# Raw up-projection weights paired by last use and loaded twice a group, third copies in another ring, operand loads on SyncE's queue

## The chip, the cores and the metric

The kernel runs on one core of a Trainium2 chip. A core has five engines, each with an instruction queue of its own that is worked through in order: TensorE (PE) for matmuls, with weight loads listed as PEld; VectorE (DVE); ScalarE (ACT); GpSimd (POOL); and SyncE (SP), which here only issues DMAs. ACT issues DMAs too; these stand in ACT's own queue between its computing instructions. The metric is device time in microseconds (us), smaller is better.

## The reference

One layer of a hybrid encoder with 2048 tokens of 1024 features, all in float32. With DEPTH = 1 only the GLA mixer runs, then a convolutional FFN:

```python
h = rmsnorm(x, mix_norm_w)
x = x + gla_mixer(h, ...)          # gated linear attention, 4 heads, chunks of 64 tokens
h = rmsnorm(x, ffn_norm_w)
u = causal_dwconv(h @ w_up, conv_w, conv_b)     # 1024 -> 5632, 3 taps over tokens
g, val = split(u, 2)                            # 2816 gate and 2816 value channels
x = x + (silu(g) * val) @ w_down                # 2816 -> 1024
out = rmsnorm(x, final_norm_w)
```

## The kernel before, in words

**Products.** float32 matmuls are made from three matmuls of high and low parts: `mm3p` (L171) issues, for each block of 128 contracted rows, high x low (L176), low x high (L177) and high x high (L178) into one PSUM bank. `split` (L181) makes the parts: ACT copies the source into the high part (L183), DVE subtracts to get the low part (L184). A 2 x 2 block product is done with seven products instead of eight (Strassen-Winograd); they are called p1 to p7, and taken in the order p1, p5, p6, p7, p4, p2, p3 (`OPS`, L86).

**Stages.** The projections of the mixer are done in four passes R, A, B, Y (Y is the out projection), for eight pairs of token tiles each, by `unit`. Pass Y adds x, and `x1_done` and `blocks` normalise and transpose the result for the FFN. For the second half of the tokens (tiles `tt >= 8`) `blocks` stores the transposed tiles to DRAM scratch `h2f` (L762), to be loaded again later. `prep_h2` makes from them the seven operands of the activations, split, and stores these to `hd` (L785). Then `phase_u(s)` is the up projection of token half s, and last the down projection over both halves.

**The up projection.** For a half, `load_op` (L842) loads the split operands of all seven products from `hd` into seven resident tiles, four DMAs of 512 KB for each, as the slot of each comes free (L846): on ACT's queue in half 0, on SP's in half 1. In half 0 these slots hold pass Y's weights until Y's last unit has used them. The weights are taken in 11 groups of two channel tiles (f = 2g and 2g + 1), each with its gate columns f and its value columns NF + f. A job is one product for one channel tile, 12 matmuls; a group has 14 jobs, tile by tile in the order of `OPS`.

The raw weights lie in a ring of four tiles of 512 KB (`raw_tile`). A channel tile's four blocks are a11 and a12 (gate columns, first and second half of the contracted rows) and a21 and a22 (value columns). In the kernel before, one tile holds a11 and a12, another a21 and a22, and `load` (L1011) fetches a group's four tiles with one DMA each (L1016), on SP except for the first group. `prep` makes the split weights of a job, five jobs ahead of its product: p1 from a11; p5 from a21 + a22 (POOL, L1026); p6 from that sum less a11 (L1029), after which a12 less the sum is formed in place (L1044) for p3; p7 from a11 - a21, formed in a21's place (L1032); p4 from a22; p2 from a12. The split weights lie in seven slots, `uw`.

p1, p6, p7 and p4 add up in one PSUM bank `ua`, p5 and p3 in one called `uc`, p2 goes to `ub`. After p1, p6 and p7 ACT copies the bank's running sum out (`copied`, L1049), and the next product of the chain must wait for that copy. The three copies, called c1, c2 and c3, come from the ring `cp` with four slots; c1 is last read after p2 (L1138), c2 after p3 (L1155), c3 right after p7 (L1145). `conv` applies the three taps (L1065 on ACT, L1067 on DVE), and `gated` multiplies gate by value (L1074), forms the operands of the down projection on POOL (L1088 to L1092) in the four-slot ring `as`, and stores them all to `ad` on SP's queue (L1078 to L1094).

**Order.** The kernel is written against a tile framework that makes the semaphores, hands out the slots of each ring and orders each engine's instructions by its own estimate of when each can start; the order in the source is a priority. What it orders on an engine is then fixed: an instruction that waits holds up all behind it on that engine. Some work (`later_do`, `spread`) is written out at times of a planner's clock that advances by 0.227 us a matmul; `spread` puts the steps of `prep_h2` for half 1 between the products of half 0, 11 us apart.

Of the kernel before, what the change touches and what calls it, by code (L numbers as in the profile page):

```python
# [10 lines left out]
F32 = mybir.dt.float32  # L11
# [5 lines left out]
P = 128  # L17
# [3 lines left out]
def f32(ap):  # L21
    return ap.bitcast(F32)
# [3 lines left out]
def hybrid_kernel(  # L26
# [17 lines left out]
    nc = tc.nc  # L44
# [14 lines left out]
    HK = KT // 2  # L59
    NF = F // P  # L60
# [25 lines left out]
    OPS = PORD = ("p1", "p5", "p6", "p7", "p4", "p2", "p3")  # L86
    NQ = NF // 2
# [19 lines left out]
    pools = {}  # L107

    def scratch(shape, name):
        return dr.tile(shape, F32, tag=name, name=name)  # L110
# [6 lines left out]
    h2f = {t: scratch([P, 2, 512], f"h2f_{t}") for t in range(TT, NTT)}  # L117
    wsd = {(ps_, o, k): scratch([P, 2, 512], f"ws_{ps_}_{o}_{k}") for ps_ in "BY" for o in ("p5", "p6", "p7", "p3") for k in range(2)}
    b12d = [scratch([P, 512], f"b12_{j}") for j in range(NP)]
    hd = {(s, o, j): scratch([P, 2, 512], f"hd_{s}_{o}_{j}") for s in range(NS) for o in OPS for j in range(PAIRS)}  # L120
    ad = {(s, o, q): scratch([P, 512], f"ad_{s}_{o}_{q}") for s in range(NS) for o in OPS for q in range(NQ)}

    def mm_ps(name):
        return ps.tile([P, 512], F32, tag="mm", name=name, bufs=4)

    def aux_ps(name):
        return ps.tile([P, 512], F32, tag="aux", name=name, bufs=4)

    def raw_tile(shape, name):
        return wr.tile(shape, F32, tag="raw", name=name, bufs=RB)  # L130

    def w_pair(name):

        return wp.tile([P, 2, 512], F32R, tag="w", name=name, bufs=WB)

    def cp_tile(name):
        return gp.tile([P, 512], F32, tag="cp", name=name, bufs=4)

    def out_tile(name):
        return gp.tile([P, 512], F32, tag="out", name=name, bufs=3)  # L140
# [21 lines left out]
    def need(*what):  # L162

        while not ready.issuperset(what):
            heapq.heappop(delayed)[-1]()
# [15 lines left out]
    def split(hi, lo, src):  # L181

        nc.scalar.copy(hi, src)  # L183
        nc.vector.tensor_sub(lo, src, f32(hi))  # L184
# [563 lines left out]
    def blocks(tt, rws):  # L748

        for k in range(2):  # L750
            pt = aux_ps(f"pt_d{tt}_{k}")
            for j in range(HK):
                kt = HK * k + j
                nc.tensor.transpose(pt[:, j * P:(j + 1) * P], rws[:, kt * P:(kt + 1) * P], ident)
            t = hb2_tile(f"hb2_{tt}_{k}", tt < TT)
            for j in range(HK):
                kt = HK * k + j
                nc.scalar.activation(t[:, j * P:(j + 1) * P], pt[:, j * P:(j + 1) * P], AF.Identity, scale=nw2[:, kt:kt + 1])
            if tt < TT:
                h2[tt, k] = t  # L760
            else:
                nc.sync.dma_start(h2f[tt][:, k, :], t)  # L762
        ready.add(f"h2f{tt}")

    def hb2_tile(name, kept):
        return yp["p"].tile([P, 512], F32, tag="hb2" if kept else "hb3", name=name, bufs=10 if kept else 2)
# [75 lines left out]
    def load_op(s, o):  # L842

        t = uh.tile([P, 2, PAIRS, 512], F32R, tag=o, name=f"h_{s}_{o}", bufs=1)
        for j in range(PAIRS):
            (nc.scalar if s == 0 else nc.sync).dma_start(f32(t[:, :, j, :]), hd[s, o, j])  # L846
        hop[o] = tuple(t[:, i].rearrange("p j (k c) -> p k j c", c=P) for i in range(2))

    ux = {}
# [152 lines left out]
    def tiles1(ap):  # L1002
        return ap.rearrange("p (j k) -> p j k", k=P)

    wuv = w_up.rearrange("(kt p) c -> p kt c", p=P)

    def phase_u(s):
        raws, wops, sums, made = {}, {}, {}, {}
        jobs = [(g, o, f) for g in range(NQ) for o in OPS for f in (2 * g, 2 * g + 1)]

        def load(g):  # L1011
            for f in (2 * g, 2 * g + 1):
                for i, c in enumerate((f, NF + f)):
                    r = raw_tile([P, 2, 512], f"ur_{s}_{c}")
                    q = nc.scalar if s == 0 and g == 0 else nc.sync
                    q.dma_start(r.rearrange("p a (k c) -> p (a k) c", c=P), wuv[:, :, c * P:(c + 1) * P])  # L1016
                    raws[f, i] = r

        def prep(k):
            g, o, f = jobs[k]  # L1020
            a11, a12 = raws[f, 0][:, 0, :], raws[f, 0][:, 1, :]
            a21, a22 = raws[f, 1][:, 0, :], raws[f, 1][:, 1, :]
            add, sub = nc.gpsimd.tensor_add, nc.gpsimd.tensor_sub
            if o == "p5":
                src = sums[f] = out_tile(f"us_{s}_{f}")
                add(src, a21, a22)  # L1026
            elif o == "p6":
                src = sums[f]
                sub(src, src, a11)  # L1029
            elif o == "p7":  # L1030
                src = a21
                sub(src, a11, a21)  # L1032
            elif o == "p3":
                src = sums.pop(f)
            else:
                src = {"p1": a11, "p2": a12, "p4": a22}[o]
            if "wx" in pools and k % (WB + WX) >= WB:
                t = pools["wx"].tile([P, 2, 512], F32R, tag="wx", name=f"uw_{s}_{f}_{o}", bufs=WX)
            else:
                t = w_pair(f"uw_{s}_{f}_{o}")  # L1040
            hl = t[:, 0, :], t[:, 1, :]
            split(hl[0], hl[1], src)
            if o == "p6":
                sub(src, a12, src)  # L1044
            wops[o, f] = hl

        def copied(name, pa):
            t = cp_tile(name)
            nc.scalar.copy(t, pa)  # L1049
            return t  # L1050
# [42 lines left out]
                last = tv  # L1093
                nc.sync.dma_start(ad[s, o, q], t)  # L1094

        load(0)
        yield
        done = 0
        bank = {}
        for k, (g, o, f) in enumerate(jobs):  # L1100
            if o == "p1" and f == 2 * g and g + 1 < NQ:
                load(g + 1)
            if s == 0 and k == 6:
                while delayed:
                    heapq.heappop(delayed)[-1]()
                yp["ctx"].close()
                pools["ctx"] = ExitStack()
                pools["us"] = pools["ctx"].enter_context(tc.tile_pool(name="us", bufs=1, reuse_waits="tile"))
                pools["wx"] = wx_ = pools["ctx"].enter_context(tc.tile_pool(name="wx", bufs=1, reuse_waits="tile"))
                spread(range(PAIRS, 2 * PAIRS), U0, U1, row_tile,  # L1110
                       lambda name: wx_.tile([P, 2, 512], F32R, tag="h2p", name=name, bufs=1))
            if s > 0 and k == 0:
                need(*(f"h2p{jj}" for jj in range(PAIRS, 2 * PAIRS)))
            if s > 0 and k < 2 * len(OPS) and k % 2 == 0:
                load_op(s, OPS[k // 2])
            if s == NS - 1 and g == NQ - 1 and f % 2 == 0:
                d_early(o)
            while done < min(len(jobs), k + (ULEAD if "wx" in pools else WB - 2) + 1):
                prep(done)
                done += 1  # L1120
            wh, wl = wops.pop((o, f))
            pairs = [((wh[:, kt * P:(kt + 1) * P], wl[:, kt * P:(kt + 1) * P]), (hop[o][0][:, kt], hop[o][1][:, kt])) for kt in range(HK)]
            if o == "p1":
                a = bank["a", f] = mm_ps(f"ua_{s}_{f}")
                mm3p(a, pairs)
                made["p1", f] = copied(f"c1_{s}_{f}", a)
            elif o == "p5":
                c = bank["c", f] = aux_ps(f"uc_{s}_{f}")
                mm3p(c, pairs)
            elif o == "p6":  # L1130
                a = bank["a", f]
                mm3p(a, pairs, first=False, more=True)
                made["u2", f] = copied(f"c2_{s}_{f}", a)
            elif o == "p2":
                pb = mm_ps(f"ub_{s}_{f}")
                mm3p(pb, pairs)
                ev, _ = new_u(0, f)
                nc.vector.tensor_add(ev, tiles1(pb), tiles1(made.pop(("p1", f))))  # L1138
            elif o == "p7":
                a = bank["a", f]  # L1140
                mm3p(a, pairs, first=False, more=True)
                u3 = copied(f"c3_{s}_{f}", a)
                ev, od = new_u(1, f)
                made["ev", f] = ev
                nc.vector.tensor_add(od, tiles1(bank["c", f]), tiles1(u3))  # L1145
            elif o == "p4":
                a = bank.pop(("a", f))
                mm3p(a, pairs, first=False, more=True)
                nc.scalar.copy(made.pop(("ev", f)), tiles1(a))
                conv(1, f)  # L1150
            else:
                c = bank.pop(("c", f))
                mm3p(c, pairs, first=False, more=True)
                _, od = tiles2(made["u", 0, f][:, 2:2 + TS])
                nc.vector.tensor_add(od, tiles1(c), tiles1(made.pop(("u2", f))))  # L1155
                conv(0, f)
                gated(f)
# [177 lines left out]
    for n, (o, s) in enumerate(units):  # L1335
# [10 lines left out]
        for q in range(NQ):  # L1346
            k = n * NQ + q
# [43 lines left out]
```

## Time and profile before

| | |
|---|---|
| median of 3 runs | 2351.18 us (2351.06 to 2351.31) |
| profiled execution | 2357.74 us, span 2356.0 us |
| mean granted TensorE clock | 0.968 |
| up projection, half 0 | 947.8 to 1451.6 us of the span |
| up projection, half 1 | 1451.6 to 1929.0 us |
| down projection and final norm | 1929.0 us to the end |
| bytes moved by DMA | 411.7 MB |

A profile line names an engine, the line of the source, the operation, what it writes and reads, and durations; `<-` after an idle time names what ended it. `q` behind an engine (SPq, ACTq) is its sequencer, which issues DMAs. Matmuls are pipelined: one lasts 0.39 us in the listing while the next starts 0.227 us later, so the spacing of starts is the cost of one.

### The profile page before, as it was taken

The page shows a single profiled execution, that of the slowest core. Times are in us where ns is not written, and L with a number is a line of the kernel's source. Part 1 is how long each engine was busy: PE and PEld are TensorE (multiplying, and loading weights), DVE is VectorE, ACT ScalarE, POOL GpSimd, SP SyncE. Part 2 cuts the span into 40 slices and gives each one's busy share as a digit, 9 for nine tenths or more (in the row PEclk, how much of TensorE's full clock was granted, in tenths as well). Part 3 has the DMA queues.
Part 4 walks back from the last instruction along what each step waited for, and adds up shares of the span by engine and source line. Part 5 has one row for each costly group of instructions (what it writes and reads, how often), then busy time and mean ns, then how long its engine had stood idle before and what let it go on. Part 6 is the DMA issues. An engine that isn't in the chain of part 4 may idle for free. (4 is left out here: it accounts for less than half of the span.)

```text
span 2356.0 us, 28886 instructions
## 1 busy us (share of the span) xinstructions
PE 2157.6 (92%) x9948; PEld 1758.3 (75%) x9948; DVE 1655.0 (70%) x2175; ACT 1106.7 (47%) x2020; POOL 700.4 (30%) x602
## 2 busy tenths in 40 slices
PE   5999899989998996987998999799999999999998
PEld 4788778877886874776776777677777778888887
DVE  7755787788778662676777777568687777556654
ACT  4454655564555772543443444344344453322333
POOL 1000111111110001454454455345555534134200
PEclk9999999999999998999999999899999999999999
DMA  6545683377457889544334428532424258554443
GB/s 202 197 160 181 212 274 120 131 250 271 156 168 230 320 316 330 179 136 146 121 103 133 149 76 268 163 87 85 116 67 125 77 200 314 170 179 158 136 163 120
DMA packets 299634, 411.74 MB, mean 175 GB/s; under 512 B 21838, under 2 KB 158206, under 8 KB 299488
## 3 DMA queue, kind: packets, MB, share of 16 engines
q1 hardware_dynamic: 263820, 351.96, 45.2%
q10 hardware_dynamic: 35668, 57.95, 7.4%
q8 instruction: 78, 1.28, 0.2%
q14 instruction: 68, 0.56, 0.1%
HBM read 266.70 MB, written 143.13 MB: 174 GB/s over the span
## 5 line engine op out<-in xcount | busy, mean ns | idle before, releaser
L176 PE MATMUL ua<-h_p,uw_p 128*128 128x512 f32 x704 | 290.4, 413 | 82.3 <-ACT c L1049 80.3
L177 PE MATMUL ua<-h_p,uw_p 128*128 128x512 f32 x704 | 286.4, 407 | 0.0
L178 PE MATMUL ua<-h_p,uw_p 128*128 128x512 f32 x704 | 285.2, 405 | 0.0
L184 DVE TENSOR_TENSOR uw_p<-ur,uw_p 128x512 fp32r<-128x512 f32 x176 | 200.7, 1174 | 106.3 <-ACT uw_p L183 106.2
L1067 DVE SCALAR_TENSOR_TENSOR t<-u,cw,t 128x1024 f32<-128x1024 f32 x176 | 264.2, 1532 | 14.7 <-ACT t L1065 14.2
L176 PE MATMUL pd_p<-dw_p,da 128*128 128x512 f32 x616 | 239.6, 389 | 0.0
L178 PE MATMUL pd_p<-dw_p,da 128*128 128x512 f32 x616 | 239.6, 389 | 0.0
L177 PE MATMUL pd_p<-dw_p,da 128*128 128x512 f32 x616 | 239.6, 389 | 0.0
L176 PEld LDWEIGHTS ua<-h_p,uw_p 128*128 128x128 f32 x704 | 138.8, 197 | 123.7 <-ACT c L1049 90.3
L184 DVE TENSOR_TENSOR da<-da_p,da 128x512 fp32r<-128x512 f32 x154 | 127.0, 876 | 109.0 <-ACT da L183 109.0
L183 ACT CAST da<-da_p 128x512 fp32r<-128x512 f32 x154 | 85.5, 618 | 209.3 <-PE pd_p L178 162.0
L183 ACT CAST uw_p<-ur 128x512 fp32r<-128x512 f32 x176 | 104.6, 617 | 147.0 <-DMA ur<-in_ffn_w_up_dram 111.8
L178 PEld LDWEIGHTS ua<-h_p,uw_p 128*128 128x128 f32 x704 | 138.7, 197 | 32.1
L177 PEld LDWEIGHTS ua<-h_p,uw_p 128*128 128x128 f32 x704 | 139.2, 198 | 31.1 <-DVE uw_p L184 0.4
L184 DVE TENSOR_TENSOR uw_p<-us,uw_p 128x512 fp32r<-128x512 f32 x132 | 111.0, 846 | 66.4 <-ACT uw_p L183 65.7
L178 PE MATMUL uc<-h_p,uw_p 128*128 128x512 f32 x352 | 138.1, 392 | 0.0
L176 PE MATMUL uc<-h_p,uw_p 128*128 128x512 f32 x352 | 138.1, 392 | 0.0
L177 PE MATMUL uc<-h_p,uw_p 128*128 128x512 f32 x352 | 138.0, 392 | 0.0
L177 PEld LDWEIGHTS pd_p<-dw_p,da 128*128 128x128 f32 x616 | 115.6, 188 | 24.1
L178 PEld LDWEIGHTS pd_p<-dw_p,da 128*128 128x128 f32 x616 | 115.6, 188 | 24.1
L176 PEld LDWEIGHTS pd_p<-dw_p,da 128*128 128x128 f32 x616 | 115.6, 188 | 23.9
L183 ACT CAST uw_p<-us 128x512 fp32r<-128x512 f32 x132 | 81.7, 619 | 110.3 <-POOL us L1029 69.6
(250 smaller groups left out, 5449.2 us busy)
## 6 DMA issues: line engine op xcount, KB each, us to landing
ur<-in_ffn_w_up_dram SPq DMA_DIRECT2D x84, 512.0 KB, 6.4
da_p<-ad_p SPq DMA_DIRECT2D x154, 256.0 KB, 3.5
hd_p<-h2p_p SPq DMA_DIRECT2D x56, 512.0 KB, 3.8
ad_p<-as_p SPq DMA_DIRECT2D x88, 256.0 KB, 2.2
ad_p<-t SPq DMA_DIRECT2D x66, 256.0 KB, 2.7
x<-in_x_dram SPq DMA_DIRECT2D x32, 512.0 KB, 5.5
ch<-in_ffn_w_down_dram SPq DMA_DIRECT2D x61, 256.0 KB, 4.9
hr_A_p<-h1d_p SPq DMA_DIRECT2D x56, 256.0 KB, 2.8
```

The lines of the kernel that those rows point to most:

```text
L176: nc.tensor.matmul(ps_ap, ah, bl, start=(first and i == 0), stop=False, **kw)
L177: nc.tensor.matmul(ps_ap, al, bh, start=False, stop=False, **kw)
L178: nc.tensor.matmul(ps_ap, ah, bh, start=False, stop=(last and i == len(pairs) - 1), **kw)
L183: nc.scalar.copy(hi, src)
L184: nc.vector.tensor_sub(lo, src, f32(hi))
L1067: nc.vector.scalar_tensor_tensor(t, u[:, k:k + TS], cw[:, k, c:c + 1], t, op0=ALU.mult, op1=ALU.add)
```

## The change

It has four parts, all of them around the up projection.

1. The raw weights of a channel tile are paired by the product that last uses them: one tile holds a11 and a21 (last used by p7), the other a22 and a12 (last used by p4 and p2). Each tile is now filled by two DMAs of 256 KB, and the next group is loaded in two portions: the a11/a21 tiles at the third job of a group, the a22/a12 tiles at its eighth. Before, all four were loaded at the first job.
2. The third copy c3 takes its slot from the ring `as` (shared with the gated sums) instead of `cp`.
3. The operand loads of half 0 (`load_op`) go to SP's queue instead of ACT's.
4. The stores of the transposed tiles to `h2f` go to ACT's queue instead of SP's.

```diff
@@ blocks
             else:
-                nc.sync.dma_start(h2f[tt][:, k, :], t)
+                nc.scalar.dma_start(h2f[tt][:, k, :], t)
@@ load_op
         for j in range(PAIRS):
-            (nc.scalar if s == 0 else nc.sync).dma_start(f32(t[:, :, j, :]), hd[s, o, j])
+            nc.sync.dma_start(f32(t[:, :, j, :]), hd[s, o, j])
@@ phase_u
-        def load(g):
+        def load(g, n):
             for f in (2 * g, 2 * g + 1):
-                for i, c in enumerate((f, NF + f)):
-                    r = raw_tile([P, 2, 512], f"ur_{s}_{c}")
+                r = raw_tile([P, 2, 512], f"ur_{s}_{f}_{n}")
+                for i, (c, k) in enumerate((((f, 0), (NF + f, 0)), ((NF + f, 1), (f, 1)))[n]):
                     q = nc.scalar if s == 0 and g == 0 else nc.sync
-                    q.dma_start(r.rearrange("p a (k c) -> p (a k) c", c=P), wuv[:, :, c * P:(c + 1) * P])
-                    raws[f, i] = r
+                    q.dma_start(r[:, i, :].rearrange("p (k c) -> p k c", c=P), wuv[:, HK * k:HK * (k + 1), c * P:(c + 1) * P])
+                raws[f, n] = r
@@ prep
-            a11, a12 = raws[f, 0][:, 0, :], raws[f, 0][:, 1, :]
-            a21, a22 = raws[f, 1][:, 0, :], raws[f, 1][:, 1, :]
+            a11, a21 = raws[f, 0][:, 0, :], raws[f, 0][:, 1, :]
+            a22, a12 = raws[f, 1][:, 0, :], raws[f, 1][:, 1, :]
@@ phase_u, the loop over jobs
-        load(0)
+        load(0, 0)
+        load(0, 1)
...
-            if o == "p1" and f == 2 * g and g + 1 < NQ:
-                load(g + 1)
+            if k % (2 * len(OPS)) in (2, 7) and g + 1 < NQ:
+                load(g + 1, int(k % (2 * len(OPS)) == 7))
...
             elif o == "p7":
                 a = bank["a", f]
                 mm3p(a, pairs, first=False, more=True)
-                u3 = copied(f"c3_{s}_{f}", a)
+                u3 = pools["us"].tile([P, 512], F32, tag="as", name=f"c3_{s}_{f}", bufs=4)
+                nc.scalar.copy(u3, a)
```

## The prediction

> **What bounds the kernel now.** I read the engine totals first, then the costliest groups, then busy time by stage, then the waits, then single groups in the timeline. From the page, TensorE (PE) and the costliest matmul group:
>
> ```profile
> PE 2157.6 (92%) x9948; PEld 1758.3 (75%) x9948; DVE 1655.0 (70%) x2175; ACT 1106.7 (47%) x2020; POOL 700.4 (30%) x602
> L176 PE MATMUL ua<-h_p,uw_p 128*128 128x512 f32 x704 | 290.4, 413 | 82.3 <-ACT c L1049 80.3
> ```
>
> PE bounds the whole, but in front of the matmuls into `ua` it sits 80.3 us, waiting for ACT's copies at L1049. Busy time by stage (columns: us, then busy us and instructions of PE, PEld, DVE, ACT, POOL, clock, DMA share, GB/s), cut at the up projection's first half, its second half's first group, the rest of that half, the down projection, and the out projection's tail:
>
> ```profile
> 947.80:1451.60 503.80, 451.06 (x1856) 362.63 (x1857) 375.77 (x370) 225.25 (x354) 246.54 (x217) 0.94 0.44 139
> 1451.60:1507.20 55.60, 41.20 (x169) 33.02 (x168) 31.99 (x31) 18.81 (x28) 22.78 (x18) 0.85 0.64 211
> 1507.20:1929.00 421.80, 394.26 (x1682) 318.49 (x1681) 321.53 (x306) 191.92 (x289) 215.37 (x159) 0.98 0.37 109
> 1929.00:2356.00 427.00, 418.92 (x1849) 346.51 (x1847) 258.03 (x329) 144.87 (x262) 113.75 (x84) 1.00 0.50 175
> 902.00:947.80 45.80, 22.83 (x78) 16.34 (x76) 6.45 (x12) 9.41 (x23) 3.30 (x4) 0.73 0.95 340
> ```
>
> Undisturbed matmuls start 0.227 us apart (first and last of 20 in a row; 4.31 / 19):
>
> ```profile
> 1300.08 0.39 PE L176 MATMUL ua<-h_p,uw_p 128*128 128x512 f32 x1
> ...
> 1304.39 0.39 PE L177 MATMUL ub<-h_p,uw_p 128*128 128x512 f32 x1
> ```
>
> A group of two channel tiles has 14 products of 12 matmuls: 168 x 0.227 = 38.1 us. Half 0 has 11 groups, 419 us, and takes 503.8: 84.6 lost. The ten later groups of half 1 need 381 and take 421.8: 40.8 lost. The down projection runs at 427 / 1849 = 0.231 us a matmul and has nothing to give. The waits of PE in half 0, then in half 1:
>
> ```profile
> PE ua L176 <- ACT c L1049: 52.7, 11, 6.5
> ...
> PE ua L176 <- ACT c L1049: 27.5, 10, 5.3
> PE ub L176 <- DMA h_p<-hd_p: 14.4, 1, 14.4
> ```
>
> What is lost beyond these waits is the slower clock after them: in half 0, 84.6 - 52.7 = 32, and the granted clock of 0.94 gives 0.06 x 503.8 = 30. One group of half 0 in the timeline, SP, then ACT, then PE:
>
> ```profile
> 1193.97 5.43 SPq L1094 DMA_DIRECT2D ad_p<-as_p  x4
> 1199.51 4.08 SPq L1016 DMA_DIRECT2D ur<-in_ffn_w_up_dram  x4
> ...
> 1203.88 0.62 ACT L183 CAST uw_p<-ur 128x512 fp32r<-128x512 f32 x1 [4.73 <-DMA ur<-in_ffn_w_up_dram]
> 1207.47 0.62 ACT L183 CAST uw_p<-ur 128x512 fp32r<-128x512 f32 x1 [2.98 <-DMA ur<-in_ffn_w_up_dram]
> 1210.45 0.62 ACT L183 CAST h2p_p<-h2r 128x512 fp32r<-128x512 f32 x1 [2.36 <-DMA h2r<-h2f]
> 1210.98 0.58 ACT L1049 COPY c<-ua 128x512 f32<-128x512 f32 x1
> ...
> 1205.36 0.39 PE L177 MATMUL ub<-h_p,uw_p 128*128 128x512 f32 x1
> 1211.61 0.79 PE L176 MATMUL ua<-h_p,uw_p 128*128 128x512 f32 x1 [5.86 <-ACT c L1049]
> ```
>
> Two faults meet. The third copy c3 needs a slot of the four-slot ring `cp`, in which c1 and c2 of both tiles still lie, so it stands behind p2's product and its addition, and p4 stands behind it. And in ACT's order it is behind the next group's first casts, which wait for raw weights that SP issued only after the gated sums' stores. The matmul after the stall takes 0.79 us, against 0.39 before it.
>
> **Part 1: c3 in the ring `as`.** c3 no longer waits for p2; it can run when p7's product ends, as c2 does after p6, and p4 of the first tile has the second tile's p7 (12 x 0.227 = 2.7 us) as cover. The copy costs ACT the same 0.58 us. The added wait: a slot of `as` comes free when a gated sum of the group before has been stored. In a group of half 1, SP and DVE:
>
> ```profile
> 1521.20 5.42 SPq L1094 DMA_DIRECT2D ad_p<-as_p  x4
> 1526.73 4.17 SPq L1016 DMA_DIRECT2D ur<-in_ffn_w_up_dram  x4
> ...
> 1519.35 7.49 DVE L184 TENSOR_TENSOR uw_p<-ur,uw_p 128x512 fp32r<-128x512 f32 x5
> ...
> 1523.91 0.59 ACT L1049 COPY c<-ua 128x512 f32<-128x512 f32 x1 [1.69 <-PE ua L178]
> ```
>
> The first two sums' stores start at 1521.2 and about 1522.9 and land 2.2 us later (median below): 1523.4 and 1525.1. The copy at 1523.91 is c2 of the second tile; p7's products follow it and end about 1526.6 and 1529.3. So the slots are 3 to 4 us early, plus 2.7 of cover: nothing. Behind the copy on ACT stand the next p1 casts and p4's own copy.
>
> **Part 2: raw weights by last use.** The page's issues, median us to landing last:
>
> ```profile
> ur<-in_ffn_w_up_dram SPq DMA_DIRECT2D x84, 512.0 KB, 6.4
> ad_p<-as_p SPq DMA_DIRECT2D x88, 256.0 KB, 2.2
> ```
>
> and, of SP's waits (total, times, longest), the longest:
>
> ```profile
> SPq L1078 <- DVE t L1074: 417.2, 21, 33.7
> ```
>
> The pair a11, a21 is dead after p7's low parts, the first of DVE's run at 1519.35, instead of after p2's, its last at 1526.84: 7 us earlier. Its four loads then land by about 1520.5 + 6.4 = 1527, and the p1 casts, which need p7's second product done for their slot (1529.3), find them. Behind a load that waits for its pair on SP stand the gated stores, for as long as DVE takes. The second pair keeps its time: it lands by 1526.8 + 6.4 = 1533, POOL reads it for p5, and PE comes to p5 eight products (p4, p2, p3, p1) after 1529.3, at 1551. The bytes are the same, in eight issues a group for four. SP's time for them is 4.2 us if it goes by bytes, 8.3 if by count (I take the latter). SP waits 417.2 / 21 = 20 us a group for the gate product alone, so this is covered; uncovered it would delay stores, not PE.
>
> **What stays.** In half 0 ACT also casts h2p, in order:
>
> ```profile
> ACT h2p_p L183 <- DMA hd_p<-h2p_p: 31.3, 9, 6.3
> ...
> ACT h2p_p L183 <- DVE h2r L790: 16.2, 2, 8.1
> ```
>
> These 11 waits, 47.5 us, are untouched. Where one lies ahead of a copy, PE has 2.7 us of cover: 47.5 - 11 x 2.7 = 17.5 us, with some half clock behind the longer ones 25, or 2.3 us a group (bounds: 0, and 47.5 / 11 = 4.3). For half 1, which has no h2p, I leave 0.6 a group, one copy (bounds: 0, and 2.1, half of today's loss of 40.8 / 10 = 4.1). Half 0: 503.8 - 11 x 40.4 = 59. Half 1: 421.8 - 10 x 38.7 = 35. The half change (55.6 us, with the 14.4 for `hd`) I leave as it is: its loads stay on SP, in an order that may move either way by that wait.
>
> **Part 3: operand loads from ACT's to SP's queue, h2f stores the other way.** ACT, then PE, at the tail of the out projection:
>
> ```profile
> 914.66 4.36 ACTq L846 DMA_DIRECT2D h_p<-hd_p  x4
> 919.06 0.62 ACT L183 CAST h_Y_p<-hr_Y_p 128x512 fp32r<-128x512 f32 x1 [4.17 <-issue]
> 919.44 6.57 ACTq L846 DMA_DIRECT2D h_p<-hd_p  x4
> ...
> 928.92 11.57 ACTq L846 DMA_DIRECT2D h_p<-hd_p  x8
> 940.54 1.06 ACT L202 ACTIVATE h<-x 128x1024 f32<-128x1024 f32 x1 [11.95 <-issue]
> ...
> 942.61 1.15 ACT L745 ACTIVATE h<-x,rstd_d 128x1024 f32<-128x1024 f32 x1 [0.92 <-POOL rstd_d L206]
> ...
> 943.81 1.97 PE L754 MATMUL pt_d<-ident,h 128*128 128x128 f32 x8 [9.84 <-ACT h L745]
> 947.80 0.80 PE L176 MATMUL ua<-h_p,uw_p 128*128 128x512 f32 x1 [2.02 <-ACT uw_p L183]
> ```
>
> ACT stands in the issue of 28 loads, and the last casts, squares and scalings of the out projection stand behind them. All 78 matmuls of this stage (row 902 to 947.8) take 17.7 us at 0.227; 28.1 of its 45.8 are lost. The chain square, root, scaling must still run (940.54 to 943.76, 3.2 us): gain 25 (bounds 0 and 28). On SP the same waits now stand ahead of x1d stores, hd stores and h2r loads, which nobody awaits within 20 us. The 16 h2f stores now follow ACT's own scaling and cost it an issue each: 0.7 us by their row on SP, 1.4 by the slowest stretch of L846 above (11.57 / 8); 11 to 23 us in all, spread over some 200 us in which PE leads, behind which stand ACT's copies and casts. I take nothing.
>
> ```profile
> 910.25 1.36 SPq L762 DMA_DIRECT2D h2f<-hb  x2
> ```
>
> Can the loads keep up? 28 x 0.524 MB at the stage's 340 GB/s are 43 us, 900 to 943, and the last operand, p3, is wanted 12 products after 923, at 955: yes, if nothing else is in their way.
>
> The Trainium skill ("DMA: Bandwidth & Descriptors", section "Issuing engines are not separate DMA queues") speaks against this part: transfers of all issuing engines share the same 16 DMA engines, and another issuer saves only issue time. By that rule the part would be worth the issue time alone and the transfers would end no sooner, so that the up projection's first group would come to wait for them; this is the second rival below. The trace agrees as far as the stage moves 340 GB/s however ACT waits; no run here shows the loads on SP in this stage.
>
> **The sum.** The profiled execution took 2357.7 (span 2356.0), 6.6 over the median of 2351.2. 2357.7 - 25 - 59 - 35 = 2238.7; less 6.6: **2232**.
>
> **Rivals.**
> *The wait moves to ACT's other in-order work.* Without stalls DVE has 375.8 / 11 = 34.2 us of work in 38.1, so casts, copies and conv terms lag; PE waits a little at c2, c3 or the low parts. For it: the two 8.1 us waits for DVE above. Against: products are prepared five ahead, 13 us. At 43 us a group in half 0 and 40.2 in half 1: 25 + 31 + 20 = 76, **2275**.
> *The operand loads set the pace.* At the half change they already do, from SP: the 14.4 us of `ub` above. The same wait in the up projection's first group, with some 2 us of half clock after it, leaves 25 - 17 = 8 of part 3: **2249**. For it: 0.95 DMA share in that stage; against: the 12 us between 943 and 955.
> *It does not do what it says:* the scheduler puts the raw loads behind the stores again and c3 behind the casts. Then only part 3 pays: **2326**; without that too, **2351**. Against: the low parts that free the first pair end before the sums' stores start.
> *The other side:* c3 now depends on a store. If SP, in order, holds a load that waits for a raw slot ahead of the `as` stores, every c3 waits for it, with p4 and ACT's next casts behind. It decides once the stores land over 5.8 us later against the products than above; slower than before from (25 + 84.6 + 40.8) / 21 = 7.2 us of PE stall a group. At 10: 2351 + 60 = **2411**. For it: SP's 417.2 us of waits in order; against: the 3 to 4 us in hand.
>
> **Chances.** Forecast 0.51, wait moves 0.20, loads set the pace 0.12, part 3 alone 0.06, nothing 0.04, slower 0.07. All of today's loss gone, with the half change's 14.4, is 2351 - 28 - 84.6 - 40.8 - 14.4 = 2183; I take 2192 below, and 2300 above to hold the first rival. Within 0.2% (4.7 us) a measurement of this kernel tells no change. Faster 0.89, same 0.04, slower 0.07.
>
> **What would show it.** Right: the wait of PE `ua` for L1049 under 20 us; groups of 38 to 41 us; ACT's waits for `ur` (4.73 and 2.98 above) gone; L846 all on SP, up projection starting near 923. Wrong: L1049 waiting for `ad` stores, PE waiting for `uw` low parts, or `ub` and `uc` waiting for `hd` in the first group.

## The result, and the profile after

The changed kernel takes 2266.0 us (median of 4 runs, 2264.7 to 2267.5) where the kernel before takes 2351.2 on the same chip: ratio 0.9628, 95% interval 0.9603 to 0.9653, or 85 us less. The forecast was 2232, so the sign and the range hold and 34 us are missing. The profiled execution took 2264.65 us with a span of 2262.9, 93.1 less span than before. The two gains differ because the profiled execution before was 6.5 us over its median, and the one after 1.4 under its own.

From the page of the changed kernel, the totals, the costliest matmul group and two rows of the DMA issues:

```profile
PE 2132.6 (94%) x9948; PEld 1744.8 (77%) x9948; DVE 1612.6 (71%) x2175; ACT 1109.8 (49%) x2020; POOL 698.5 (31%) x602
...
L176 PE MATMUL ua<-h_p,uw_p 128*128 128x512 f32 x704 | 284.3, 404 | 42.5 <-ACT c L1145 31.9
...
ur<-in_ffn_w_up_dram SPq DMA_DIRECT2D x168, 256.0 KB, 3.4
...
hd_p<-h2p_p SPq DMA_DIRECT2D x56, 512.0 KB, 3.2
```

The idle time before `ua` has halved (82.3 to 42.5), and what ends it is now the copy at L1145, which is c3 (c1 and c2 are copied at L1050). Busy time by stage of the changed kernel, with the columns of the prediction (us, then busy us and instructions of PE, PEld, DVE, ACT, POOL, clock, DMA share, GB/s): out projection's tail, half 0, first group of half 1, its other ten, down projection.

```profile
902.00:918.60 16.60, 12.79 (x49) 10.21 (x50) 6.54 (x9) 6.30 (x15) 5.58 (x5) 0.90 1.04 368
918.60:1401.10 482.50, 444.58 (x1865) 359.04 (x1864) 361.74 (x373) 229.01 (x357) 250.48 (x221) 0.96 0.49 162
1401.10:1449.80 48.70, 42.81 (x174) 34.44 (x173) 29.93 (x32) 19.15 (x29) 22.87 (x19) 0.93 0.71 241
1449.80:1834.45 384.65, 384.65 (x1677) 314.36 (x1676) 290.77 (x303) 192.79 (x289) 205.37 (x155) 1.00 0.38 118
1834.45:2262.90 428.45, 419.18 (x1848) 346.42 (x1847) 261.62 (x328) 143.92 (x261) 119.15 (x86) 0.99 0.51 175
```

Against the stages before:

| stage | before | after | gained | forecast |
|---|---|---|---|---|
| start of the up projection | 947.8 | 918.6 | 29.2 | 25 |
| half 0, 11 groups | 503.8 | 482.5 | 21.3 | 59 |
| first group of half 1 | 55.6 | 48.7 | 6.9 | 0 |
| ten later groups of half 1 | 421.8 | 384.65 | 37.1 | 35 |
| down projection, end | 427.0 | 428.45 | -1.4 | 0 |

The gains add up to 93.1. In the ten later groups PE is busy for 384.65 of 384.65 us at clock 1.00: 38.5 us a group, nothing left to take. Half 0 is what falls short of the forecast, by 38 us. There PE waits for c3, and ACT waits for a store, not for weights (waits of the changed kernel within half 0: total, times, longest):

```profile
ACT h2p_p L183 <- DMA hd_p<-h2p_p: 56.1, 19, 8.3
...
PE ua L176 <- ACT c L1145: 31.9, 8, 5.2
...
ACT uw_p L183 <- DMA x1d<-x: 10.1, 1, 10.1
...
PE ua L176 <- ACT c L1050: 4.7, 1, 4.7
...
ACT uw_p L183 <- DMA ur<-in_ffn_w_up_dram: 0.6, 1, 0.6
```

One such wait in the timeline of the changed kernel:

```profile
1074.36 1.79 DVE L184 TENSOR_TENSOR h2p_p<-h2r,h2p_p 128x512 fp32r<-128x512 f32 x1
...
1075.63 5.43 SPq L1095 DMA_DIRECT2D ad_p<-as_p  x4
...
1081.15 2.09 SPq L1017 DMA_DIRECT2D ur<-in_ffn_w_up_dram  x4
...
1083.29 0.49 SPq L785 DMA_DIRECT2D hd_p<-h2p_p  x1
...
1089.73 0.62 ACT L183 CAST h2p_p<-h2r 128x512 fp32r<-128x512 f32 x1 [8.29 <-DMA hd_p<-h2p_p]
1090.26 0.58 ACT L1145 COPY c<-ua 128x512 f32<-128x512 f32 x1
...
1090.89 0.79 PE L176 MATMUL ua<-h_p,uw_p 128*128 128x512 f32 x1 [5.20 <-ACT c L1145]
```

Half 1's operand is finished by DVE at 1076.15. Its store stands on SP behind the four gated sums and the four loads of the second raw pair, is issued at 1083.29, and lands 6.3 us later (page's median 3.2). The next operand's cast needs the slot; c3 of the second tile is behind that cast in ACT's order, and p4 behind c3. (A group takes each product for both of its tiles before the next product.) Of PE's eight waits for c3 in half 0, seven stand like this one right behind an h2p cast that waited 5.9 to 8.3 us for the store. The chain is not new: before, these casts waited 31.3 us, and there too the store stood behind the four sums and the raw loads (four stores of sums from 1052.81, four loads from 1058.35, the store at 1062.56, and ACT's wait of 5.95 us until 1069.24). The waits have grown; the run c3_queues below shows that it takes no new load for that.

### The profile page after: what moved, and what is told of

Read it like the earlier page. It is cut to its first block, busy times and chain, and to the rows that moved or that the text cites. A ratio compares the mean times of both kernels' runs of the same rounds, so it can differ in the third digit from the quotient of the medians.

```text
span 2262.9 us, 29154 instructions
## 1 busy us (share of the span) xinstructions
PE 2132.6 (94%) x9948; PEld 1744.8 (77%) x9948; DVE 1612.6 (71%) x2175; ACT 1109.8 (49%) x2020; POOL 698.5 (31%) x602
## 4 chain that ended last, share of the span: by engine, by line
PE 65%; DVE 12%; DMA 10%; ACT 5%; issue 4%; POOL 3%; SPq 1%; ACTq 0%; DVEq 0%; POOLq 0%
PE ua L176 5%; PE ua L177 5%; PE ua L178 5%; PE pd_p L177 5%; PE pd_p L178 5%; PE pd_p L176 5%; PE uc L178 3%; PE uc L176 3%; PE uc L177 3%; PE mp_R L176 2%; DVE t L1068 2%; PE mp_R L177 2%; PE mp_R L178 2%; PE mp_Y L176 2%; DMA hd_p<-h2p_p 2%
## 5 line engine op out<-in xcount | busy, mean ns | idle before, releaser
L176 PE MATMUL ua<-h_p,uw_p 128*128 128x512 f32 x704 | 284.3, 404 | 42.5 <-ACT c L1145 31.9
L177 PE MATMUL ua<-h_p,uw_p 128*128 128x512 f32 x704 | 282.3, 401 | 0.0
L178 PE MATMUL ua<-h_p,uw_p 128*128 128x512 f32 x704 | 281.8, 400 | 0.0
L1068 DVE SCALAR_TENSOR_TENSOR t<-u,cw,t 128x1024 f32<-128x1024 f32 x176 | 250.9, 1427 | 13.2 <-ACT t L1066 12.4
L184 DVE TENSOR_TENSOR uw_p<-ur,uw_p 128x512 fp32r<-128x512 f32 x176 | 162.9, 940 | 64.8 <-ACT uw_p L183 56.8
L184 DVE TENSOR_TENSOR da<-da_p,da 128x512 fp32r<-128x512 f32 x154 | 135.4, 932 | 98.9 <-ACT da L183 98.8
L176 PEld LDWEIGHTS ua<-h_p,uw_p 128*128 128x128 f32 x704 | 136.2, 194 | 77.0 <-ACT c L1145 35.3
L178 PEld LDWEIGHTS ua<-h_p,uw_p 128*128 128x128 f32 x704 | 136.2, 194 | 30.9
L177 PEld LDWEIGHTS ua<-h_p,uw_p 128*128 128x128 f32 x704 | 136.7, 194 | 30.2
L184 DVE TENSOR_TENSOR uw_p<-us,uw_p 128x512 fp32r<-128x512 f32 x132 | 119.1, 909 | 56.5 <-ACT uw_p L183 55.2
L1066 ACT ACTIVATE t<-u,cw 128x1024 f32<-128x1024 f32 x88 | 109.7, 1247 | 53.8 <-DVE u L1158 53.8
```

Source lines behind the costliest of these rows:

```text
L176: nc.tensor.matmul(ps_ap, ah, bl, start=(first and i == 0), stop=False, **kw)
L177: nc.tensor.matmul(ps_ap, al, bh, start=False, stop=False, **kw)
L178: nc.tensor.matmul(ps_ap, ah, bh, start=False, stop=(last and i == len(pairs) - 1), **kw)
L1066: nc.scalar.activation(t, u[:, 2:2 + TS], AF.Identity, scale=cw[:, 2, c:c + 1], bias=cw[:, 3, c:c + 1])
L1068: nc.vector.scalar_tensor_tensor(t, u[:, k:k + TS], cw[:, k, c:c + 1], t, op0=ALU.mult, op1=ALU.add)
```

## The experiments

Medians, and ratios to the kernel before timed on the same chip with 95% intervals. "Half 0" and "end" (of half 0, us of the span) come from the profiled execution.

| run | median | ratio | half 0 | end |
|---|---|---|---|---|
| before | 2351.2 | 1 | 503.8 | 1451.6 |
| after | 2266.0 | 0.9628 (0.9603-0.9653) | 482.5 | 1401.1 |
| only_c3 | 2282.2 | 0.9687 (0.9670-0.9705) | 461.4 | 1404.5 |
| only_raw | 2324.3 | 0.9862 (0.9845-0.9878) | 496.9 | 1444.7 |
| only_queues | 2348.9 | 0.9966 (0.9951-0.9980) | 525.5 | 1445.8 |
| c3_queues | 2270.5 | 0.9660 (0.9639-0.9681) | 474.5 | 1394.6 |
| x1d_act | 2263.1 | 0.9634 (0.9610-0.9657) | 475.6 | 1402.6 |
| no_h2p | 2221.7 | 0.9436 (0.9420-0.9452) | 431.7 | 1355.1 |
| hd_act | 2252.0 | 0.9562 (0.9544-0.9579) | 463.0 | 1387.7 |
| hd_pool | 2283.7 | 0.9694 (0.9673-0.9715) | 493.9 | 1422.3 |
| wx2 | 2263.7 | 0.9628 (0.9612-0.9644) | 470.0 | 1398.0 |
| wx2_h2p2 | 2257.5 | 0.9603 (0.9588-0.9617) | 462.7 | 1384.5 |
| hd_act_h2p2 | 2256.8 | 0.9584 (0.9566-0.9602) | 460.6 | 1380.3 |
| cast_pool | 2264.4 | 0.9633 (0.9606-0.9661) | 476.2 | 1398.2 |

**Each part alone.** The kernel before with c3 moved, with the raw pairing, and with the two queue edits.

```diff
only_c3:
-                u3 = copied(f"c3_{s}_{f}", a)
+                u3 = pools["us"].tile([P, 512], F32, tag="as", name=f"c3_{s}_{f}", bufs=4)
+                nc.scalar.copy(u3, a)
only_raw: load(g, n), its two call sites and the pairing in prep, nothing else
only_queues:
-                nc.sync.dma_start(h2f[tt][:, k, :], t)
+                nc.scalar.dma_start(h2f[tt][:, k, :], t)
-            (nc.scalar if s == 0 else nc.sync).dma_start(f32(t[:, :, j, :]), hd[s, o, j])
+            nc.sync.dma_start(f32(t[:, :, j, :]), hd[s, o, j])
```

> The kernel before with the third copies in the ring of the gated sums, nothing else. If the slot of c3 was the fault (it had to wait for p2's addition), the copy now stands ahead of the next group's casts on ACT and half 1's groups fall from 41 to about 38.6 us: 37 us there and some 20 in half 0, 2294 in all. If the late raw weights were the fault, ACT still stands in the casts that wait for them before it comes to c3, and at most 10 us are gained: 2341 or more.

> The kernel before with the raw weights paired by last use and loaded twice a group, nothing else. If the slot of c3 was the fault, c3 still waits for p2's addition and PE for c3: groups of half 1 near 40 us, 2335 or more. If the late raw weights were the fault, ACT's waits for them go and with them most of the stall: 2295.

> The kernel before with the operand loads on SP's queue and the h2f stores on ACT's, nothing else. If ACT's standing in the issue of the loads was the loss at the out projection's tail, the up projection starts 25 to 29 us earlier: 2322 to 2326. If the transfers set the pace and only issue time is saved: 2334 or more.

c3's slot is worth 74 us alone, the pairing 32, the queues 7. Each expectation names two cases. The gain of only_c3 is above the 57 us of its first, only_raw lies between its two, and only_queues lies in the second (2334 or more) although the up projection starts as early as the first case has it. The three add up to 113 and the whole gives 85. Most of the overlap is in half 1 (columns as above; half 0, half change and the ten later groups of only_c3, then of only_raw):

```profile
943.10:1404.50 461.40, 439.82 (x1856) 355.82 (x1857) 367.06 (x367) 223.48 (x352) 254.20 (x216) 0.97 0.46 147
1404.50:1457.80 53.30, 41.27 (x170) 32.96 (x169) 34.72 (x37) 20.60 (x31) 27.07 (x22) 0.87 0.79 269
1457.80:1843.90 386.10, 386.06 (x1682) 315.25 (x1681) 302.64 (x295) 186.53 (x282) 208.23 (x151) 1.00 0.38 112
```

```profile
947.80:1444.70 496.90, 448.12 (x1856) 361.22 (x1857) 369.26 (x370) 226.76 (x353) 252.54 (x217) 0.95 0.43 138
1444.70:1501.20 56.50, 40.96 (x169) 32.86 (x168) 32.88 (x31) 19.46 (x29) 23.07 (x19) 0.85 0.71 242
1501.20:1895.50 394.30, 389.11 (x1682) 316.19 (x1682) 330.75 (x306) 193.24 (x289) 221.16 (x159) 0.99 0.38 116
```

Either edit alone brings half 1's groups to 38.6 us (only_raw nine of the ten, its last 46.4): the stall needed both faults. There the two edits gain 35.7 and 27.5 us alone and 37.1 in the changed kernel, mostly the same time twice. In half 0 it is c3 that pays (42.4 us; the pairing 6.9). With c3 in its new ring PE also runs p4 right behind p7; before, 19 matmuls of p2 stand between.

only_queues starts the up projection at 920.3, 27.5 earlier, and then takes 21.7 longer for half 0: its first two groups need 50.4 and 52.0 us (43.2 and 47.4 before), which is 11.8 of them. In the first group PE waits for a row that ACT scales late, behind GpSimd (POOL), which had stood in a wait for raw weights (timeline of only_queues, POOL and PE):

```profile
924.24 1.26 POOL L1026 TENSOR_TENSOR us<-ur 128x512 f32<-128x512 f32 x1 [23.27 <-DMA ur<-in_ffn_w_up_dram]
...
929.81 1.97 PE L754 MATMUL pt_d<-ident,h 128*128 128x128 f32 x8 [5.92 <-ACT h L745]
```

**What the pairing adds to the rest.** The kernel before with c3 and the queues, without the pairing.

```diff
-                u3 = copied(f"c3_{s}_{f}", a)
+                u3 = pools["us"].tile([P, 512], F32, tag="as", name=f"c3_{s}_{f}", bufs=4)
+                nc.scalar.copy(u3, a)
... and the two edits of only_queues
```

> The changed kernel with the raw weights paired and loaded as before: c3 in the other ring and the queues exchanged, no more. If c3's slot made the gain, half 1's ten later groups stay at 386 us, half 0 is no longer than the changed kernel's 482, and the time is within 8 us of the changed kernel's 2266. If the pairing has a share of its own behind c3, the time is 2280 or more.

0.9660 against 0.9628, with intervals that overlap: what the pairing adds is not told apart from nothing. The run keeps within 8 us of the changed kernel, as its first case has it. By the profile half 0 ends 6.5 us earlier without the pairing, and the half change, cut at the same matmul, is 7.9 longer (56.6 against 48.7). Without it some copies do wait for their new ring; waits of c3_queues in half 0:

```profile
ACT c L1143 <- DMA ad_p<-as_p: 12.6, 4, 4.5
...
PE ua L176 <- ACT c L1143: 0.8, 1, 0.8
```

PE pays 0.8 us for these 12.6, so the rival on the other side had its mechanism but not its price. In the changed kernel no copy waits for a sum's store at all.

c3_queues loads the raw weights as before, and yet its h2p casts wait 69.8 us for the store in half 0 (18 times), more than the changed kernel's 56.1; in only_c3 it is 62.5 (16 times). One of these waits in the timeline of c3_queues, SP, then ACT:

```profile
1073.72 5.43 SPq L1094 DMA_DIRECT2D ad_p<-as_p  x4
1079.25 2.50 SPq L1016 DMA_DIRECT2D ur<-in_ffn_w_up_dram  x3
1081.81 1.78 SPq L785 DMA_DIRECT2D hd_p<-h2p_p  x1
...
1090.79 0.62 ACT L183 CAST h2p_p<-h2r 128x512 fp32r<-128x512 f32 x1 [9.96 <-DMA hd_p<-h2p_p]
```

In only_raw it is 54.9 (11 times), in only_queues 45.8 (15 times). So the waits grow with each of the edits by itself, and the new place of the raw loads is not needed for it. Why they grow was not tested.

**The first groups.** The changed kernel with the last x1 stores on ACT's queue.

```diff
-        nc.sync.dma_start(x1d[t], xt)
+        (nc.scalar if t + 2 >= NTT else nc.sync).dma_start(x1d[t], xt)
```

> The changed kernel with the x1d stores of the last two token tiles on ACT's queue. Theory: in the up projection's first group ACT's cast waits 10.1 us for such a store, which SP issues only behind the operand loads, because the split weights' new slots lie where that tile lay; then the wait goes, group 0 falls from 47.6 to 42 us, and the time is 2256 to 2262. Rival: the wait is for whatever frees that memory last, such as the h2f stores: the same wait under another name, 2264 to 2268.

The timeline of the changed kernel shows what this removes: the up projection begins, ACT's first split cast waits.

```profile
918.60 0.39 PE L176 MATMUL ua<-h_p,uw_p 128*128 128x512 f32 x1
...
921.52 1.06 ACT L202 ACTIVATE h<-x 128x1024 f32<-128x1024 f32 x1
...
940.50 3.53 SPq L846 DMA_DIRECT2D h_p<-hd_p  x4
944.13 0.54 SPq L742 DMA_DIRECT2D x1d<-x  x1
...
952.40 0.62 ACT L183 CAST uw_p<-us 128x512 fp32r<-128x512 f32 x1 [10.11 <-DMA x1d<-x]
953.55 0.50 PE L176 MATMUL ua<-h_p,uw_p 128*128 128x512 f32 x1 [3.75 <-ACT c L1145]
```

The last x1 tile is ready by 921.5, where ACT reads it. Its store stands behind the last operand loads on SP until 944.13, and ACT waits for that store until 952.4, with c3 behind it. With the store on ACT that wait is gone and group 0 takes 41.3 us for 47.6, as its theory had it. But the up projection starts at 927.0, 8.4 later, and the total does not change (0.9634, interval 0.9610 to 0.9657; 2263.1 us lies between its two cases). At its tail PE now waits once for a cast (timeline of x1d_act); why the cast is late was not followed further.

```profile
914.45 1.22 PE L176 MATMUL mp_Y<-w_Y_p,h_Y_p 128*128 128x512 f32 x2 [5.18 <-ACT h_Y_p L183]
```

**What half 0 still loses.** no_h2p leaves out the preparation of half 1's operands, and half 1 multiplies half 0's. Its loads of operands stay; what goes is that preparation's loads, casts, differences and stores.

```diff
-            nc.sync.dma_start(f32(t[:, :, j, :]), hd[s, o, j])
+            nc.sync.dma_start(f32(t[:, :, j, :]), hd[0, o, j])
-                spread(range(PAIRS, 2 * PAIRS), U0, U1, row_tile, ...)
-            if s > 0 and k == 0:
-                need(*(f"h2p{jj}" for jj in range(PAIRS, 2 * PAIRS)))
```

> The changed kernel without the preparation of half 1's operands: no h2r loads, h2p casts and hd stores in half 0; half 1 multiplies half 0's operands instead, so half 1's FFN is computed from the wrong tokens. If the h2p casts are all that half 0 loses beyond its first two groups, its groups from the third on take 38.6 us as half 1's do, half 0 falls from 482 to some 435, and the time is 2220 to 2230 (VectorE, ACT and DMA have less work too). If VectorE's or ACT's own load or the order of the raw loads holds it, groups stay over 41 us and the time is 2245 or more.

Half 0 of no_h2p (columns as above):

```profile
923.40:1355.10 431.70, 427.08 (x1865) 348.02 (x1865) 331.24 (x329) 212.47 (x328) 271.27 (x220) 1.00 0.43 135
```

From the third group on every group takes 38.6 us. So the preparation costs half 0 50.8 us (482.5 - 431.7), and no other cause is needed for those groups. All of this came as the first case of its expectation had it. The changed kernel says the same: its groups take 44 to 50 us until the last store of the preparation is issued at 1273.3, and 38.6 after. The next runs ask which part of it costs.

**The store.** The same kernel as changed, with the store of half 1's operands issued by ACT, or by GpSimd (hd_pool, with `nc.gpsimd` in the same place).

```diff
-                nc.sync.dma_start(hd[s, o, j], f32(hl))
+                (nc.scalar if s else nc.sync).dma_start(hd[s, o, j], f32(hl))
```

> The changed kernel with half 1's hd stores (L785) on ACT's queue instead of SP's. First theory: half 0 still loses 58 us because each h2p cast waits for the one h2p slot, whose store SP issues only behind the gated sums' stores and the raw loads, and c3 stands behind that cast on ACT. Then the store issues some 8 us earlier, the waits of PE for c3 (31.9 us) go, and the time is 2215 to 2230. Rival: VectorE is what is late in half 0 (34 us of work in a 38 us group); then ACT waits for its low parts at the store instead, and the time stays within 2258 to 2275.

> The changed kernel with half 1's hd stores on GpSimd's queue: issued early as on ACT's, but ACT waits for no low part. If late issue is the cause, half 0 is at most as long as with the stores on ACT (463 us) and the time 2240 to 2252. If GpSimd's own work, now held up behind the stores, delays the sums for p5 and p6, it is 2255 or more.

**A second slot.** It needs space: wx2 has a split-weight ring of 2 for 3 (the first line), wx2_h2p2 also two slots for the operand, hd_act_h2p2 also the store on ACT.

```diff
-    WX = 3
+    WX = 2
-                       lambda name: wx_.tile([P, 2, 512], F32R, tag="h2p", name=name, bufs=1))
+                       lambda name: wx_.tile([P, 2, 512], F32R, tag="h2p", name=name, bufs=2))
```

> The changed kernel with six slots for split weights instead of seven (WX = 2), the control for the next run. Products are still prepared ahead, so 0 to 15 us more: 2266 to 2281.

> The same with two slots for h2p instead of one, in the room that WX = 2 leaves. If the one slot, freed late by a store, is what half 0 still loses, ACT's waits before h2p casts fall from 56 us to under 15 and the time is 25 to 45 us under the control. If VectorE is late in half 0, it is within 8 us of the control.

> Half 1's hd stores on ACT's queue and two h2p slots (in the room of WX = 2) together. Either alone left 32 to 35 us of ACT's waits for these stores. If late issue and the one slot both count, the waits fall under 12 us and the time is 2235 to 2247. If ACT's standing before the store for VectorE's low part takes their place, it stays at 2250 or more.

Waits within half 0, first of hd_pool, then of hd_act, then of hd_act_h2p2 (and two rows of its timeline, ACT and PE):

```profile
ACT h2p_p L183 <- DMA hd_p<-h2p_p: 79.2, 16, 10.9
...
PE ua L176 <- ACT c L1050: 44.4, 9, 9.1
```

```profile
ACT h2p_p L183 <- DMA hd_p<-h2p_p: 31.6, 18, 3.5
...
PE ua L176 <- ACT c L1050: 21.4, 9, 9.5
```

```profile
PE ua L176 <- ACT c L1050: 20.0, 7, 4.6
...
ACT c L1050 <- DVE h2p_p L184: 12.1, 4, 4.6
ACT h2p_p L183 <- DMA hd_p<-h2p_p: 11.1, 8, 2.1
```

```profile
989.08 0.58 ACT L1050 COPY c<-ua 128x512 f32<-128x512 f32 x1 [4.62 <-DVE h2p_p L184]
...
989.72 0.79 PE L176 MATMUL ua<-h_p,uw_p 128*128 128x512 f32 x1 [4.63 <-ACT c L1050]
```

With the wait for the store at 79, 56 (the changed kernel), 32 and 11 us, half 0 ends at 1422, 1401, 1388 and 1380. (The end is compared, since the up projection's start varies from 918.6 to 928.4 among these runs.) The wait for the store is therefore a cause, and cutting it brings the end of half 0 forward by about 20 us: the last 45 us of it bring 21 (18 against wx2, which has hd_act_h2p2's smaller ring). It also paces the preparation: the last store is issued at 1273.3 in the changed kernel, at 1213.0 in hd_act and at 1165.0 in hd_act_h2p2, and in all three the groups take some 38.5 us behind that point and 40 to 52 ahead of it, the first aside.

Against the expectations:

- hd_act (2252.0) lies between its two cases. PE's waits for c3 go from 31.9 to 5.9 us, but those for c1 and c2 rise from 4.7 to 21.4. It is 0.9562 against 0.9628, with intervals apart: 15 us by the ratio. It is the fastest of the kernels that do the whole work, though not told apart from hd_act_h2p2.
- hd_pool has the time of its second case and not its mechanism: ACT's waits for GpSimd's sums stay (50.4 us for 50.8). GpSimd, too, comes late to the store (58.5 us of waits there for the low parts, and its own sums ahead of it).
- wx2 costs nothing (2263.7, just under its expectation).
- wx2_h2p2 still waits 35.3 us for the store where under 15 were expected, and gains 6 us for 25 to 45 (0.9603 against 0.9628 for wx2, intervals that overlap a little).
- hd_act_h2p2 has the waits that were expected (11.1) and not the time: 2256.8 lies in its second case, and the new wait of that case is there. ACT's copies wait 12.1 us behind a store that waits for VectorE's low part, and PE's longest wait for a copy, c1 or c2, follows at once (the two rows above).

So of the 46 us by which no_h2p ends half 0 earlier, some 25 remain in hd_act_h2p2, but not all of these are free of the store: a part is the wait that the store brought to ACT. One cure stands untried: in the source the store of an operand is written at the start of the next step, beside the cast that waits for it (`store` in `step`), and no run wrote it right behind its own difference.

**The cast's place.** The high part of half 1's operands on GpSimd instead of ACT.

```diff
-            split(hl[:, 0, :], hl[:, 1, :], ts[n])
+            if s:
+                nc.gpsimd.tensor_copy(hl[:, 0, :], ts[n])
+                nc.vector.tensor_sub(hl[:, 1, :], ts[n], f32(hl[:, 0, :]))
+            else:
+                split(hl[:, 0, :], hl[:, 1, :], ts[n])
```

> Against the changed kernel (2266.0; half 0 482.5 us, of which no_h2p took away 51). Only this differs: the high part of half 1's operands is cast on GpSimd instead of ScalarE; the stores, the slot and the low part on VectorE stay. If half 0 loses only because the cast that waits for the store stands ahead of c2's and c3's copies in ScalarE's order, the wait moves to GpSimd, whose 250 us in half 0 (23 of 44 a group) leave it room: ScalarE's waits for the store (56.1 us) go to zero, PE's waits for the copies fall from 36.6 to under 12, half 0 takes 440 to 460, and the whole 2225 to 2245. If GpSimd has no room for a wait of that length, the sums p5 and p6 behind it come late, ScalarE waits for GpSimd before its casts of the sums, PE for those or the copies behind them: half 0 stays above 475 and the whole is 2255 or more.

Waits of cast_pool in half 0:

```profile
ACT uw_p L183 <- POOL us L1034: 92.1, 21, 6.5
...
DVE h2p_p L796 <- POOL h2p_p L795: 56.0, 16, 7.1
...
PE ua L176 <- ACT c L1054: 31.0, 9, 5.7
...
POOL h2p_p L795 <- DMA hd_p<-h2p_p: 20.3, 8, 3.7
```

No change in the time (0.9633), and half 0 takes 476.2 us: both lie in the second case. ACT no longer waits for the store, but its waits for GpSimd's sums rise from 50.8 to 92.1 us, and PE's waits for the copies go from 36.6 only to 34.4. VectorE waits 56.0 us for the cast on GpSimd (47.4 in the changed kernel, for the cast on ACT), and ACT in turn 50.6 us at L1156 for VectorE's addition behind it, where it had no such wait. So taking the cast off ACT does not cure the loss: the wait moves with the work, through GpSimd and VectorE, back to ACT's copies. The run does not show that the cast's place on ACT was harmless. What stays open is how the rest divides between the store's new waits and the preparation's differences on DVE (361.7 us busy in half 0 for 331.2 without it), its casts and its loads; no run separated them.

## Why the prediction was right or wrong

**Right: half 1.** Forecast 387 us for ten groups, measured 384.65. The two faults, c3's slot and the casts' late weights, were the cause; the runs add that curing one is enough, which the prediction did not see. The 0.6 us a group that it left for waiting did not come: PE has no wait in these ten groups, and the undisturbed group itself takes 38.5 us where the prediction had 38.1. That the two nearly cancel is luck. **Right: c3's new ring costs nothing.** The forecast had the slots 3 to 4 us early. In the timeline of the changed kernel, half 1:

```profile
1500.07 5.09 SPq L1095 DMA_DIRECT2D ad_p<-as_p  x4
...
1506.77 0.59 ACT L1145 COPY c<-ua 128x512 f32<-128x512 f32 x1 [1.73 <-issue]
1509.49 0.59 ACT L1145 COPY c<-ua 128x512 f32<-128x512 f32 x1 [1.61 <-issue]
```

The first store, at 1500.07, lands by 1502.3 with the page's 2.2 us; c3 comes at 1506.77, 4.5 us later. **Right: the casts find their weights.** Their waits for `ur` in half 0 are 0.6 us (45.5 before). SP's time for eight issues a group was a choice between 4.2 us by bytes and 8.3 by count; four take 2.09 us (row 1081.15), so 4.2 it is. But bytes are not shown to be the reason: the quickest such issue on SP takes 0.37 us for 512 KB (before) and for 256 KB (after), and the median 0.66 and 0.50.

**Near in size, wrong in its credit: the tail.** The up projection starts 29.2 us earlier, for 25 (bounds 0 and 28, so just above the upper one). The step that failed is "on SP the same waits now stand ahead of x1d stores, hd stores and h2r loads, which nobody awaits within 20 us". The x1d store was ready 23 us before its issue, and a split-weight slot awaited it: 10.1 us on ACT, 3.75 on PE. In only_queues the tail's 27.5 shrink to 7 in the total. The Trainium skill ("DMA: Bandwidth & Descriptors", section "Issuing engines are not separate DMA queues") says that DMAs of all issuing engines run on the same 16 DMA engines and that issuing from several engines saves only the time it takes to issue. The trace agrees: the last operand load is issued at 945.4 before, on ACT, and at 943.4 after, on SP. What left the path was ACT's own work behind the issues. The net of 7 is near what the rival "the operand loads set the pace" gave part 3 (8), but by luck: its wait of `ub` measured only 0.5 us, and what only_queues loses in its first group is a wait behind GpSimd (5.92 us, above). What the x1 store costs the whole is not shown: x1d_act took its wait away and the total stayed, but the up projection also started 8.4 us later there.

**Wrong: half 0, the term "what stays".** The prediction left the waits before h2p's casts "untouched", 2.3 us a group (bounds 0 and 4.3), 25 us in all. Half 0 took 43.9 us a group for the forecast 40.4, and lost 482.5 - 419 = 63 us, 5.8 a group, above the upper bound. By no_h2p this is 50.8 us for the preparation, 7 in the first two groups, which had no term, and 5 to 6 because an undisturbed group takes 38.6 us and not 38.1. Two errors stand in the 25. The waits were not untouched: those for the store grew from 31.3 us in 9 to 56.1 in 19, and each edit alone makes them grow (45.8 to 62.5 us), so why they do is open. And they are not the whole: with 11.1 us of them left, 25 us of the loss remain, and I had priced only these waits, not the preparation's work in order on full engines. How much of the 25 is that work is open.

**The rivals.** "The wait moves to ACT's other in-order work" came nearest (2275): its 43 us a group in half 0 is nearly what was measured (43.9), though the copies come late behind casts that wait for a store, not because DVE lags. Its 40.2 in half 1 is wrong: nothing lags there, and half 0 runs as fast without the preparation. Part 3 alone, nothing, and slower did not occur. The half change gained 6.9 us that I had left at zero. Neither the pairing nor c3 with the queues gives them alone (56.5 in only_raw, 56.6 in c3_queues, 55.6 before); the changed kernel, with all parts, takes 48.7. Of "what would show it", the `ua` wait under 20 us (36.6) and groups of 38 to 41 (half 0: 44 to 50, the last three 38.6) came out against the forecast, in half 0 alone.

## What to carry to other kernels

When a transfer is added to or moved past an in-order queue, follow each store behind it to the slot that it frees, then to the instruction that needs the slot, and to what stands behind that one in its engine's order; "nobody reads it soon" is no answer where a buffer is reused. Cost two cures of one stall together, not each alone: in half 1 either removed it. Price a piece of background work by leaving it out, not by adding up its waits: here the waits gave 25 us and leaving it out showed 50.8. And where moving such work to another engine leaves the total as it was, follow the wait: here it came back through two other engines.

## What the runs showed of the hardware

The last operand load was issued at 945.4 us on ACT's queue and at 943.4 on SP's, and from 902 to 946 us the DMA share was 0.95 before and 0.96 after, at 338 and 341 GB/s. So another queue did not move these transfers faster; it changed who stands behind them. And a 512 KB store issued right behind four 256 KB loads took 6.3 us to land (row 1083.29), twice the median of 3.2. This is one such store.
